# Layer 0's first MLP matmul by seven products of halves, sums in place of the raw weights, and one modulation vector handed to layer 1

## The chip, the cores and the metric

The kernel runs on one core of one Trainium2 chip. The metric is the device time of one execution in microseconds (us). The engines are TensorE (PE in the profile; PEld is its weight load), VectorE (DVE), ScalarE (ACT), GpSimd (POOL) and SyncE (SP), whose queue issues the weight transfers.

## The reference

Two layers act on 128 context tokens and 512 latent tokens, 640 in all, with a model width of 1024. Layer 0 mixes by attention, layer 1 by a gated delta rule; each then has a squared-ReLU MLP with 4096 hidden columns. Six modulation vectors a layer (shift, scale and gate, for the mixer and for the MLP) come from a conditioning vector, one set for context and one for latent tokens. Everything is float32.

```python
m = jax.nn.silu(cvec) @ w + b            # modulation: w is 1024 x 6144
def squared_relu_mlp(h, w1, w2):
    return jnp.square(jax.nn.relu(h @ w1)) @ w2
for layer in range(2):
    sh1, sc1, g1, sh2, sc2, g2 = modulation(c, mod_w, mod_b)
    x = x + g1 * mixer(rms_norm(x, norm1) * (1 + sc1) + sh1)
    x = x + g2 * squared_relu_mlp(rms_norm(x, norm2) * (1 + sc2) + sh2, mlp_w1, mlp_w2)
```

## The kernel before

Activations are stored transposed, features on partitions, the 640 tokens along the free axis in two halves of 320. A float32 product is three matmuls of parts rounded to fp32r: high by high, high by low and low by high (lines 245 to 247). The 16 activation tiles `act` hold the high and low parts of the normalised input.

`dense` multiplies by a weight matrix in groups of 512 output columns. A block of 128 columns and one half of the tokens takes 8 x 3 = 24 matmuls into a bank of PSUM (`dn` and `p1` by turns). Weights come in transfers of 1 MB for 256 columns, all 1024 rows (`fetch`, line 255), into two raw buffers by turns. `split_w` makes the high part by a ScalarE copy (line 228) and the low part by a VectorE subtraction (line 229) in four pairs of buffers, used in rotation: `hls`, named `t`, and the pair `wxh`, `wxl`.

Modulation is hidden under the matmuls. `mod_steps` is a generator: each step fetches 1 MB of `mod_w` and folds it on VectorE into two accumulators `ma` (line 190 for the first, line 192 for the others, four operations a step); after four steps eight matmuls (line 198, `pick`) sum over the partitions, and two transposes and two additions store the vector. `fill(n)` runs n such steps from the list `fillers`, and `dense` calls it at every weight fetch.

The program is issued from this code. In the part from layer 0's output projection on, the tile framework keeps the order by engine, except that it moves an instruction ahead where another has to wait by its own estimate; so what one loop yields is interleaved with what others yield.

The MLP goes through four quarters of 1024 hidden columns: `w1` for a quarter (hidden tiles `hh`, `hl` by `split_h`, lines 542 and 543), then `w2` for it, which adds into the residual (line 407). In layer 1 the second to fourth quarters of `w1` go through `seven`: per 256 columns the inputs and the weights are cut into 2 x 2 halves (features by tokens, columns by features), and Strassen's product in Winograd's form takes 7 products of 12 matmuls, 84, in place of 96. The input sums T1 to T4 are made once (`sums`). The weight sums S1 to S4 are made for each tile by `forms`, one step of it after every second product (`tile_of`); `kept` copies a partial product from PSUM (line 472), `put` adds the last one to it (line 482), and `ev7` applies the squared ReLU, on VectorE for one of four results (line 553) and on ScalarE otherwise (lines 555 and 556). Layer 0's MLP is plain `dense` in all quarters, with `fill=1` at each fetch: its seven pending vectors are layer 0's last, (0, 5), and layer 1's (1, 0) to (1, 5).

At the entry of each MLP the second half of the tokens is still being normalised: `sumsq` accumulates squares (line 299), a matmul by ones (line 306) sums them over partitions, and lines 383 to 395 scale and split.

Of the kernel before, what the change touches and what calls it, by code (L numbers as in the profile page):

```python
# [49 lines left out]
class Net:  # L50
# [211 lines left out]
    def dense_steps(self, w, row0, col0, ncol, xs, evac, tag=("dn", "dn"), fill=0, wide=(), size=4, between=None, early=None):  # L262


        for q in range(0, ncol, size * P):
# [4 lines left out]
            for i, (b, hf) in enumerate(steps):  # L270
                if b not in ws:
                    t = col0 + b * P
                    ws[b], ws[b + 1] = self.ahead.pop((w.tensor.name, row0, t), None) or self.fetch(w, row0, t)
                    self.fill(fill)
# [138 lines left out]
    def seven(self, pool):  # L413
# [10 lines left out]
        def sums():  # L424
            for k in range(4):
                b = []
                for z in (act(k, 0), act(k, 1), act(k + 4, 0), act(k + 4, 1)):
                    t = pool.tile([P, TH], F32, tag="c", name="b", bufs=4)
# [10 lines left out]
        def forms(w, col0):  # L439
# [5 lines left out]
            z = self.split_w(raw[:, :, 0:P], [P, NK, P])  # L445
            f["11"], f["12"] = ([y[:, 4 * i:4 * i + 4] for y in z] for i in range(2))
            yield f
            t = pool.tile([P, 2, 4, P], F32, tag="s0", name="s", bufs=1)
            nc.vector.tensor_tensor(out=t[:, 0], in0=a21, in1=a22, op=ALU.add)
            nc.vector.tensor_tensor(out=t[:, 1], in0=t[:, 0], in1=a11, op=ALU.subtract)  # L450
            z = self.split_w(t.rearrange("p a k c -> p (a k) c"), [P, NK, P])
            f["S1"], f["S2"] = ([y[:, 4 * i:4 * i + 4] for y in z] for i in range(2))
            yield f
            u = pool.tile([P, 2, 4, P], F32, tag="s1", name="s", bufs=1)
            nc.vector.tensor_tensor(out=u[:, 0], in0=a11, in1=a21, op=ALU.subtract)
            nc.vector.tensor_tensor(out=u[:, 1], in0=a12, in1=t[:, 1], op=ALU.subtract)
            z = self.split_w(u.rearrange("p a k c -> p (a k) c"), [P, NK, P])
            f["S3"], f["S4"] = ([y[:, 4 * i:4 * i + 4] for y in z] for i in range(2))
            yield f
            f["22"] = self.split_w(a22, [P, 4, P])  # L460
# [14 lines left out]
        def tile_of(f, nxt, out):  # L475
# [4 lines left out]
            def put(i, hf, ps, sb, op=ALU.add):  # L480
                c = pool.tile([P, TH], F32, tag="c", name="c", bufs=4)
# [15 lines left out]
            u3 = kept(a, "k4")  # L497
# [6 lines left out]
            put(1, 0, u3, c, ALU.subtract)  # L504
# [23 lines left out]
    def mlp(self, layer, xs, last, fill=0, between=None, early=None, fast=None):  # L528

        nc, tc = self.nc, self.tc  # L530
        with ExitStack() as c:
            hp = c.enter_context(tc.tile_pool(name="hp", bufs=16 if fast else 20))
            rp = c.enter_context(tc.tile_pool(name="rp", bufs=4))
            w1, w2 = self.i[f"mlp_w1_{layer}"], self.i[f"mlp_w2_{layer}"]
            for ch in range(4):
# [15 lines left out]
                def ev7(fb, hf, h):  # L551
                    if fb % 2 == 0 and hf == 0:
# [1174 lines left out]
```

## Time and profile before

| | us |
|---|---|
| median of three runs (lowest and highest) | 1848.47 (1845.96, 1849.6) |
| profiled execution | 1845.21 |
| span of its profile, first to last instruction | 1843.5 |
| mean granted TensorE clock of that span | 0.987 of full |
| TensorE, VectorE, ScalarE busy | 1754.1, 1208.7, 851.5 |
| first matmul of layer 1's second seven-product stage, and of the plain stage after it | 1521.33, 1570.61 |

All other numbers on the trace are from the profiled execution and count from the start of its span. Busy times are shares of the whole span, and the stages differ, so a stage has to be read by itself. In the timeline a matmul's length overlaps the next one's, since matmuls are pipelined; the distance of starts is the pace.

### The profile page before, as it was taken

The numbers are of one execution on the slowest core, as the hardware profiler recorded it, in microseconds if no ns is written. First come the engines' busy times: TensorE is split into PE (matmuls) and PEld (weight loads), VectorE is DVE, ScalarE is ACT, GpSimd is POOL, SyncE is SP. The second block draws the span as 40 slices with busy tenths as digits, with TensorE's granted clock in tenths as the row PEclk, the third lists the DMA queues.
The fourth block names the chain that finished last, engine by engine and source line by source line (L and its number), as shares of the span: only waits on it lengthen the run. The fifth ranks groups of instructions, "written<-read, shape, count | busy, mean of one in ns | idle before, by whom it ended". The sixth has DMA issues, their size and how long they took to land. (4 is left out here: it accounts for less than half of the span.)

```text
span 1843.5 us, 34925 instructions
## 1 busy us (share of the span) xinstructions
PE 1754.1 (95%) x14264; PEld 1648.8 (89%) x14264; DVE 1208.7 (66%) x2420; ACT 851.5 (46%) x1877; POOL 254.0 (14%) x252
## 2 busy tenths in 40 slices
PE   5899998899999999999989999999999999999999
PEld 4898876699999999999878888888899999999999
DVE  6766557478676667745687877776447757465562
ACT  4555576335223132233665666656645426254360
POOL 1233314111000000001331222222112000000000
PEclk8999998999999999999999999999999999999999
DMA  9201059324444344532223222222241212222131
GB/s 330 70 27 49 25 169 270 126 91 140 154 165 138 137 139 142 178 99 78 78 67 76 55 48 48 69 70 59 79 135 46 92 46 92 92 69 92 60 109 50
DMA packets 174992, 187.22 MB, mean 102 GB/s; under 512 B 48456, under 2 KB 152136, under 8 KB 174832
## 3 DMA queue, kind: packets, MB, share of 16 engines
q1 hardware_dynamic: 170272, 175.05, 30.2%
q0 software_dynamic: 1408, 5.41, 0.9%
q10 hardware_dynamic: 3152, 4.52, 0.7%
q8 instruction: 112, 1.84, 0.4%
q14 instruction: 48, 0.39, 0.1%
HBM read 170.97 MB, written 11.37 MB: 99 GB/s over the span
## 5 line engine op out<-in xcount | busy, mean ns | idle before, releaser
L228 ACT CAST t<-t 128x1024 fp32r<-128x1024 f32 (+1 forms) x151 | 152.7, 1013 | 250.3 <-PE p L246 152.5
L245 PE MATMUL dn<-t 128*128 128x320 f32 x792 | 252.6, 319 | 4.8 <-PEq L78 3.1
L246 PE MATMUL dn<-t 128*128 128x320 f32 x792 | 253.3, 320 | 1.3 <-DVE t L395 0.8
L247 PE MATMUL dn<-t 128*128 128x320 f32 x792 | 252.0, 318 | 0.0
L229 DVE TENSOR_TENSOR t<-t 128x1024 fp32r<-128x1024 f32 (+1 forms) x151 | 179.2, 1188 | 76.7 <-ACT t L228 76.5
L245 PEld LDWEIGHTS dn<-t 128*128 128x128 f32 x792 | 149.9, 189 | 9.1 <-issue 5.4
L246 PEld LDWEIGHTS dn<-t 128*128 128x128 f32 x792 | 149.9, 189 | 5.9 <-issue 2.5
L247 PEld LDWEIGHTS dn<-t 128*128 128x128 f32 x792 | 149.9, 189 | 3.3 <-issue 2.5
L246 PE MATMUL p<-hl,t 128*128 128x320 f32 x448 | 138.4, 309 | 0.0
L407 DVE SCALAR_TENSOR_TENSOR x<-p,t,x 128x192 f32<-128x192 f32 (+2 forms) x154 | 53.3, 386 | 128.5 <-PE p L247 128.5
L192 DVE SCALAR_TENSOR_TENSOR ma<-t,ma 128x1024 f32<-128x1024 f32 x98 | 123.3, 1279 | 13.7 <-DMA t<-in_mod_w_dram 13.7
L246 PE MATMUL dn<-hl,t 128*128 128x320 f32 x416 | 128.5, 309 | 0.0
L245 PE MATMUL p<-hh,t 128*128 128x320 f32 x392 | 121.1, 309 | 0.0
L247 PE MATMUL p<-hh,t 128*128 128x320 f32 x392 | 121.1, 309 | 0.0
L245 PE MATMUL dn<-hh,t 128*128 128x320 f32 x376 | 116.4, 310 | 0.0
L247 PE MATMUL dn<-hh,t 128*128 128x320 f32 x376 | 116.2, 309 | 0.0
L388 POOL TENSOR_TENSOR nt<-x,rs 128x320 f32<-128x320 f32 x30 | 31.0, 1048 | 567.7 <-ACT rs L308 538.0
L245 PE MATMUL p<-t 128*128 128x320 f32 x344 | 108.2, 314 | 0.0
L247 PE MATMUL p<-t 128*128 128x320 f32 x344 | 107.3, 312 | 0.0
L246 PE MATMUL p<-t 128*128 128x320 f32 x344 | 107.2, 312 | 0.0
L228 ACT CAST wxh<-t 128x1024 fp32r<-128x1024 f32 x43 | 45.1, 1048 | 103.0 <-PE p L246 60.0
L246 PEld LDWEIGHTS p<-hl,t 128*128 128x128 f32 x448 | 84.1, 188 | 0.0
(568 smaller groups left out, 5017.1 us busy)
## 6 DMA issues: line engine op xcount, KB each, us to landing
t<-in_mlp_w_dram SPq DMA_DIRECT2D x64, 1024.0 KB
t<-in_mod_w_dram SPq DMA_DIRECT2D x40, 1024.0 KB, 7.6
t<-in_w_qkv_dram SPq DMA_DIRECT2D x12, 1024.0 KB
t<-in_w_in_dram SPq DMA_DIRECT2D x9, 1024.0 KB, 5.4
w<-in_mod_w_dram SPq DMA_DIRECT2D x4, 2048.0 KB, 15.5
t<-in_w_out_dram SPq DMA_DIRECT2D x8, 1024.0 KB, 5.5
bias<-in_biasx_dram SPq DMA_DIRECT2D x8, 512.0 KB, 8.1
t<-in_w_z_dram SPq DMA_DIRECT2D x4, 1024.0 KB
```

Of the source, the lines that this page charges most:

```text
L192: nc.vector.scalar_tensor_tensor(out=acc[v], in0=wt[:, k], scalar=c, in1=acc[v], op0=ALU.mult, op1=ALU.add)
L228: nc.scalar.copy(hi, raw)
L229: nc.vector.tensor_tensor(out=lo, in0=raw, in1=hi.bitcast(F32), op=ALU.subtract)
L245: self.nc.tensor.matmul(ps, lhsT=hi[:, k, :], rhs=xh[:, ts_], start=(k == 0), stop=False)
L246: self.nc.tensor.matmul(ps, lhsT=hi[:, k, :], rhs=xl[:, ts_], start=False, stop=False)
L247: self.nc.tensor.matmul(ps, lhsT=lo[:, k, :], rhs=xh[:, ts_], start=False, stop=(k == NK - 1))
L388: nc.gpsimd.tensor_tensor(out=t, in0=xt[k][:, c], in1=rs[:, c], op=ALU.mult)
L407: nc.vector.scalar_tensor_tensor(out=xout[:, a:b], in0=ps[:, a - o:b - o], scalar=self.mod_vec(layer, idx, k, v), in1=xin[:, a:b], op0=ALU ...
```

## The change

Both layers now run the same MLP. Quarter 0 of `w1` is plain, with one modulation step at each fetch; in its `w2` stage the input sums are made, one k-pair at each fetch, and the other three quarters of `w1` go through `seven`. In layer 0 the modulation steps at `w2`'s fetches go by turns of 1, 1 and 2 and there are none in the seven-product stages; layer 0 makes the vectors (0, 5) and (1, 0) to (1, 4), and (1, 5) is made at the entry of layer 1's MLP, in quarter 0 of `w1`.

In `forms` the sums are written over the raw weights (only S1's operand has a buffer of its own, `s`), and the splits are grouped otherwise: a11 and a12 together, S1 alone, S2 and S4, then S3 and a22; before it was S1 with S2, S3 with S4, and a22 alone. In `tile_of` the last result now takes its partial product from PSUM and a kept copy of the other, so that three kept tags are used in place of four. `ev7` is always two ScalarE operations. Buffers move between pools: `c` has 3 in place of 4, `hp` of layer 0 has 16 in place of 20, and the pool of the normalisation is closed while `sv` is open and opened again for the last `w2`.

```diff
-                    self.fill(fill)
+                    fill() if callable(fill) else self.fill(fill)

...
-                    t = pool.tile([P, TH], F32, tag="c", name="b", bufs=4)
+                    t = pool.tile([P, TH], F32, tag=("c", "c", "c", "k1")[len(b)], name="b", bufs=(3, 3, 3, 1)[len(b)])

...
-            z = self.split_w(raw[:, :, 0:P], [P, NK, P])
-            f["11"], f["12"] = ([y[:, 4 * i:4 * i + 4] for y in z] for i in range(2))
+
+            def split(i, *names):
+                z = self.split_w(raw[:, :, i * P:(i + 1) * P], [P, NK, P])
+                for j, nm in enumerate(names):
+                    f[nm] = [y[:, 4 * j:4 * j + 4] for y in z]
+
+            split(0, "11", "12")
             yield f
-            t = pool.tile([P, 2, 4, P], F32, tag="s0", name="s", bufs=1)
-            nc.vector.tensor_tensor(out=t[:, 0], in0=a21, in1=a22, op=ALU.add)
-            nc.vector.tensor_tensor(out=t[:, 1], in0=t[:, 0], in1=a11, op=ALU.subtract)
-            z = self.split_w(t.rearrange("p a k c -> p (a k) c"), [P, NK, P])
-            f["S1"], f["S2"] = ([y[:, 4 * i:4 * i + 4] for y in z] for i in range(2))
+            t = pool.tile([P, 4, P], F32, tag="s", name="s", bufs=1)
+            for out, u, v, op in ((t, a21, a22, ALU.add), (a21, a11, a21, ALU.subtract), (a11, t, a11, ALU.subtract),
+                                  (a12, a12, a11, ALU.subtract)):
+                nc.vector.tensor_tensor(out=out, in0=u, in1=v, op=op)
+            f["S1"] = self.split_w(t, [P, 4, P])
             yield f
-            u = pool.tile([P, 2, 4, P], F32, tag="s1", name="s", bufs=1)
-            nc.vector.tensor_tensor(out=u[:, 0], in0=a11, in1=a21, op=ALU.subtract)
-            nc.vector.tensor_tensor(out=u[:, 1], in0=a12, in1=t[:, 1], op=ALU.subtract)
-            z = self.split_w(u.rearrange("p a k c -> p (a k) c"), [P, NK, P])
-            f["S3"], f["S4"] = ([y[:, 4 * i:4 * i + 4] for y in z] for i in range(2))
+            split(0, "S2", "S4")
             yield f
-            f["22"] = self.split_w(a22, [P, 4, P])
+            split(1, "S3", "22")
...
-                c = pool.tile([P, TH], F32, tag="c", name="c", bufs=4)
+                c = pool.tile([P, TH], F32, tag="c", name="c", bufs=3)

...
-            u3 = kept(a, "k4")
             put(1, 1, a, s5)
             product(d, f["S4"], x["22"], False, True)
             put(0, 1, d, u2)
             step()
             c = self.bank("p1")[:, 0:TH]
             product(c, f["22"], x["T4"], True, True)
-            put(1, 0, u3, c, ALU.subtract)
+            put(1, 0, a, kept(c, "k2"), ALU.subtract)
             step()
...
         return sums(), columns
-    def mlp(self, layer, xs, last, fill=0, between=None, early=None, fast=None):
+    def mlp(self, layer, xs, last, fill=0, between=None, early=None, room=None, back=None):
         nc, tc = self.nc, self.tc
         with ExitStack() as c:
-            hp = c.enter_context(tc.tile_pool(name="hp", bufs=16 if fast else 20))
+            hp = c.enter_context(tc.tile_pool(name="hp", bufs=16))
             rp = c.enter_context(tc.tile_pool(name="rp", bufs=4))
+            sv = c.enter_context(ExitStack())
             w1, w2 = self.i[f"mlp_w1_{layer}"], self.i[f"mlp_w2_{layer}"]
             for ch in range(4):
                 hs = {}
...
-                    if fb % 2 == 0 and hf == 0:
-                        nc.vector.scalar_tensor_tensor(out=h, in0=h, scalar=0.0, in1=h, op0=ALU.max, op1=ALU.mult)
-                    else:
-                        nc.scalar.activation(h, h, AF.Relu)
-                        nc.scalar.activation(h, h, AF.Square)
+                    nc.scalar.activation(h, h, AF.Relu)
+                    nc.scalar.activation(h, h, AF.Square)
                     split_h(fb, hf, h)
 
-                if ch and fast:
+                if ch:
                     columns(w1, ch * D, 4, ev7)
+                    fill2 = fill
                 else:
-                    self.dense(w1, 0, ch * D, D, xs, ev1, tag=("dn", "p1"), fill=fill, wide=(0,) if ch == 0 else (), early=early if ch == 0 else None)
-                    if fast:
-                        fast()
-                        sums, columns = self.seven(c.enter_context(tc.tile_pool(name="sv", bufs=1)))
-                        self.fillers.insert(0, sums)
-                self.dense(w2, ch * D, 0, D, hs, lambda k, hf, ts_, ps: last(k, hf, ps, ch), tag=("dn", "p1"), fill=1 if fast and not ch else fill,
+                    self.dense(w1, 0, 0, D, xs, ev1, tag=("dn", "p1"), fill=1, wide=(0,), early=early)
+                    room()
+                    sums, columns = self.seven(sv.enter_context(tc.tile_pool(name="sv", bufs=1)))
+
+                    def fill2():
+                        next(sums, None)
+                        fill()
+
+                if ch == 3:
+                    sv.close()
+                    if back:
+                        back()
+                self.dense(w2, ch * D, 0, D, hs, lambda k, hf, ts_, ps: last(k, hf, ps, ch), tag=("dn", "p1"), fill=fill2,
                            wide=(1,) if ch == 3 and between else (), between=between if ch == 3 else None)
-                if fast:
-                    self.fill(99)
 
 
 def attn_layer(n):
...
-            n.open_norm(cn)
-            n.modp = cn.enter_context(n.tc.tile_pool(name="mp", bufs=1))
+            n.modp = cn.enter_context(n.tc.tile_pool(name="mp", bufs=1, side="right"))
+            nn = ctx.enter_context(ExitStack())
+            n.open_norm(nn, side="right")
...
-            n.fillers += [n.mod_steps(l, j, "s1") for l, j in [(0, 5)] + [(1, j) for j in range(6)]]
+            n.fillers += [n.mod_steps(l, j, "s1") for l, j in [(0, 5)] + [(1, j) for j in range(5)]]
             def last0(k, hf, ps, ch):
...
-            n.mlp(0, xs, last0, fill=1, between=between0, early=(1, lambda: n.norm_half(x0, 0, 1, 1)))
+            turns = cycle((1, 1, 2))
+            n.mlp(0, xs, last0, fill=lambda: n.fill(next(turns)), between=between0, early=(1, lambda: n.norm_half(x0, 0, 1, 1)),
+                  room=nn.close, back=lambda: n.open_norm(nn, side="right"))
             def before():
+                nn.close()
+                cn.close()
-                cn.close()
...
+            n.modp = cn.enter_context(n.tc.tile_pool(name="mp", bufs=1, side="right"))
+            n.fillers.append(n.mod_steps(1, 5, "s1"))
             def last1(k, hf, ps, ch):
-            n.mlp(1, xs, last1, early=(1, lambda: n.norm_half(x2, 1, 1, 1)), fast=cn.close)
-            cn.close()
+            n.mlp(1, xs, last1, fill=lambda: n.fill(1), early=(1, lambda: n.norm_half(x2, 1, 1, 1)), room=cn.close)
```

Line numbers of the changed kernel are one or two higher around `seven` (`kept` is 473, `put` 483, relu and square 554 and 555, `hh` 544).

On ScalarE, one steady tile of a seven-product stage (the `w1` of layer 1), in the order before. `k` are the kept copies from the banks `dn` and `s`, `t<-s 128x1024` is the high part of two sums, `c` a result on its way to `hh`.

```order
L472 COPY k_18004<-dn 128x320
L542 CAST hh<-c 128x320
L228 CAST t<-s 128x1024
L472 COPY k_18019<-s_18006 128x320
L472 COPY k_18038<-dn 128x320
L555 ACTIVATE c<-c 128x320
L556 ACTIVATE c<-c 128x320
L228 CAST t<-s 128x1024
L542 CAST hh<-c 128x320
L555 ACTIVATE c<-c 128x320
L228 CAST t<-t 128x512
L556 ACTIVATE c<-c 128x320
```

The same engine and place in the changed kernel:

```order
L473 COPY k_19187<-dn 128x320
L555 ACTIVATE c<-c 128x320
L544 CAST hh<-c 128x320
L228 CAST wxh<-t 128x1024
L554 ACTIVATE c<-c 128x320
L555 ACTIVATE c<-c 128x320
L473 COPY k_19224<-dn 128x320
L544 CAST hh<-c 128x320
L228 CAST t<-s 128x512
L473 COPY k_19239<-s_19226 128x320
L554 ACTIVATE c<-c 128x320
L555 ACTIVATE c<-c 128x320
```

The copy of 512 elements now stands first among the sums (S1, from `s`) and the wide ones come from the raw buffer `t`; a relu and a square go with every result.

On VectorE at the entry of layer 1's MLP, before: L407 is the residual update of `w_out1`, L299 the sum of squares, L383 and L393 the normalisation.

```order
L407 SCALAR_TENSOR_TENSOR x_15998<-dn,t,x_15998 128x320
L299 TENSOR_TENSOR acc<-acc,sq 128x320
L407 SCALAR_TENSOR_TENSOR x_16000<-p_16342,t,x_16000 128x320
L299 TENSOR_TENSOR acc<-acc,sq 128x320
L383 SCALAR_TENSOR_TENSOR nt<-x_15986,t,rs 128x320
L393 TENSOR_SCALAR nt<-nt,t 128x320
```

And in the changed kernel:

```order
L299 TENSOR_TENSOR acc<-acc,sq 128x320
L190 TENSOR_SCALAR ma<-t 128x1024
L192 SCALAR_TENSOR_TENSOR ma<-t,ma 128x1024 x2
L407 SCALAR_TENSOR_TENSOR x_16180<-dn,t,x_16180 128x320
L299 TENSOR_TENSOR acc<-acc,sq 128x320
L407 SCALAR_TENSOR_TENSOR x_16182<-p_16524,t,x_16182 128x320
L299 TENSOR_TENSOR acc<-acc,sq 128x320
L192 SCALAR_TENSOR_TENSOR ma<-t,ma 128x1024
L383 SCALAR_TENSOR_TENSOR nt<-x_16168,t,rs 128x320
```

The first modulation step of (1, 5) now stands between the last residual updates, one operation of it directly ahead of the first normalisation (another L190 stands one row above this piece).

On TensorE, the picks of one of layer 0's vectors before, at the end of a half-block of `w1` (`p`), with the next block's matmuls (`dn`) behind them:

```order
L247 MATMUL p_6714<-t 128x320
L198 MATMUL s_6754<-ma,t 32x256 x8
L245 MATMUL dn<-t,wxh 128x320
L246 MATMUL dn<-t,wxh 128x320
L247 MATMUL dn<-t,wxl 128x320
```

And in the changed kernel the picks of a vector in the `w2` stage of quarter 2:

```order
L245 MATMUL dn<-hh,t 128x320
L198 MATMUL s_9384<-ma,t 32x256 x4
L246 MATMUL dn<-hl,t 128x320
L247 MATMUL dn<-hh,t 128x320
L245 MATMUL dn<-hh,t 128x320
L246 MATMUL dn<-hl,t 128x320
L247 MATMUL dn<-hh,t 128x320
L245 MATMUL dn<-hh,t 128x320
L246 MATMUL dn<-hl,t 128x320
L247 MATMUL dn<-hh,t 128x320
L198 MATMUL s_9384<-ma,t 32x256 x4
L245 MATMUL p_9429<-hh,t 128x320
```

The eight picks are now two groups of four inside and at the end of a half-block, eight matmuls apart. TensorE has 144 matmuls of 320 columns fewer in the whole program; the counts of SP and POOL are the same.

## Rows read from the trace of the kernel before

**Rows 1.** The page's first part: engine, busy us, share of the span, instructions.

```profile
PE 1754.1 (95%) x14264; PEld 1648.8 (89%) x14264; DVE 1208.7 (66%) x2420; ACT 851.5 (46%) x1877; POOL 254.0 (14%) x252
```

**Rows 2.** Windows: PE, PEld, DVE, ACT, POOL busy (count), granted clock, DMA share, GB/s.

```profile
460.00:860.00 400.00, 400.00 (x2780) 395.32 (x2779) 258.54 (x367) 107.13 (x177) 0.00 (x0) 1.00 0.43 141
1521.00:1571.00 50.00, 50.00 (x343) 50.00 (x342) 35.18 (x57) 34.13 (x67) 0.00 (x0) 1.00 0.31 98
```

**Rows 3.** TensorE's timeline at stage starts: start, length, instruction, idle before.

```profile
1521.33 0.46 PE L467 MATMUL dn<-t,wxh 128*128 128x320 f32 x2
...
1570.61 0.31 PE L245 MATMUL dn<-hh,wxh 128*128 128x320 f32 x1
...
1627.26 0.46 PE L467 MATMUL dn<-t,wxh 128*128 128x320 f32 x2
```

**Rows 4.** TensorE's timeline in layer 0's MLP: first picks of two successive vectors.

```profile
456.37 0.42 PE L198 MATMUL s<-ma,t 128*32 128x256 f32 x4
...
514.09 0.42 PE L198 MATMUL s<-ma,t 128*32 128x256 f32 x4
```

**Rows 5.** TensorE's timeline at both MLP entries: layer 0, then layer 1.

```profile
394.18 0.54 PE L306 MATMUL s<-acc,t 128*128 128x320 f32 x1
...
413.11 0.82 PE L306 MATMUL s<-acc,t 128*128 128x320 f32 x1 [2.29 <-DVE acc L299]
...
1390.39 0.51 PE L306 MATMUL s<-acc,t 128*128 128x320 f32 x1
...
1410.05 1.44 PE L306 MATMUL s<-acc,t 128*128 128x320 f32 x2 [3.04 <-DVE acc L299]
...
1450.93 0.31 PE L245 MATMUL dn<-t 128*128 128x320 f32 x1
```

**Rows 6.** VectorE by shape, 400 to 860 us: busy, mean ns, idle before.

```profile
L192 DVE SCALAR_TENSOR_TENSOR ma<-t,ma 128x1024 f32<-128x1024 f32 x95 | 119.5, 1279 | 12.2 <-DMA t<-in_mod_w_dram 12.2
...
L190 DVE TENSOR_SCALAR ma<-t 128x1024 f32<-128x1024 f32 x12 | 9.0, 750 | 3.9 <-PE s L198 3.9
```

**Rows 7.** Windows behind the two waits of rows 5.

```profile
413.00:423.00 10.00, 9.89 (x55) 9.50 (x56) 10.00 (x18) 7.50 (x16) 3.00 (x4) 0.83 0.53 179
1410.00:1420.00 10.00, 9.95 (x56) 9.55 (x57) 7.93 (x17) 6.14 (x16) 3.83 (x4) 0.83 0.34 107
```

**Rows 8.** ScalarE by shape, 1521 to 1571 us, a seven-product stage.

```profile
L542 ACT CAST hh<-c 128x320 fp32r<-128x320 f32 x14 | 6.4, 457 | 1.4 <-DVE c L553 1.3
...
L555 ACT ACTIVATE c<-c 128x320 f32<-128x320 f32 x11 | 5.1, 468 | 3.4 <-DVE c L482 3.4
L472 ACT COPY k<-dn 128x320 f32<-128x320 f32 x12 | 5.1, 422 | 7.2 <-PE dn L467 7.2
L556 ACT ACTIVATE c<-c 128x320 f32<-128x320 f32 x10 | 4.7, 470 | 0.1
L228 ACT CAST wxh<-t 128x1024 fp32r<-128x1024 f32 x4 | 4.2, 1051 | 1.5 <-PE p L467 1.4
...
L228 ACT CAST t<-t 128x512 fp32r<-128x512 f32 x3 | 1.8, 606 | 0.0
```

**Rows 9.** VectorE by shape, 1521 to 1571 us.

```profile
L543 DVE TENSOR_TENSOR hl<-c,hh 128x320 fp32r<-128x320 f32 x13 | 6.3, 486 | 1.8 <-ACT hh L542 1.8
L229 DVE TENSOR_TENSOR wxl<-t,wxh 128x1024 fp32r<-128x1024 f32 x4 | 4.9, 1218 | 0.0
...
L229 DVE TENSOR_TENSOR t<-t 128x512 fp32r<-128x512 f32 x3 | 2.1, 690 | 0.0
...
L482 DVE TENSOR_TENSOR c<-dn,k 128x320 f32<-128x320 f32 x4 | 1.9, 487 | 0.1
```

**Rows 10.** VectorE's timeline behind that stage's end.

```profile
1574.11 0.49 DVE L543 TENSOR_TENSOR hl<-c,hh 128x320 fp32r<-128x320 f32 x1 [0.34 <-ACT hh L542]
```

**Rows 11.** What line 192 waits for (us, times), and the modulation transfers (median us to landing).

```profile
  DMA t<-in_mod_w_dram: 13.7, 18
...
t<-in_mod_w_dram SPq DMA_DIRECT2D x40, 1024.0 KB, 7.6
```

More of the change, by code (lines that the diff above doesn't have):

```diff
@@ L1 @@
 import math
-from itertools import chain
+from itertools import chain, cycle
 from contextlib import ExitStack, contextmanager
```

## The prediction

> **What bounds the kernel now.** I read the page's first part, then busy time by windows, then single matmuls in TensorE's timeline, then VectorE and ScalarE by shape, and last the waits and transfers of the weights. The first part says that TensorE is busy for 95% of the span and VectorE for 66% [rows 1]. The windows say what that average hides: from 460 to 860 us, layer 0's MLP, TensorE is busy for 400.00 of 400 us, and from 1521 to 1571 us, a stage of layer 1 that already works with seven products, for 50.00 of 50, both at full clock [rows 2]. So inside both MLPs time is the number of matmuls, as long as VectorE, ScalarE and the weights keep up. The pace is read from two starts: the stage that begins at 1521.33 ends where a plain one begins, at 1570.61 [rows 3]. It holds 4 tiles of 7 products of 12 matmuls, 336, so one takes 49.28 / 336 = 0.1467 us. The plain stage after it (8 blocks, 2 halves, 24 matmuls: 384) and the next boundary end at 1627.26: 56.65 against 384 x 0.1467 = 56.32. The boundary loses 0.33 us; from the first number to the third one quarter is 105.93.
>
> **Matmuls removed.** Three quarters of layer 0's first matmul go from 384 matmuls to 336, 144 fewer in all: 144 x 0.1467 = -21.1 us. Nothing lies beside these, since TensorE has no idle time there; all of it is on the path, and this is also the floor.
>
> **New boundaries.** Layer 0 gets three transitions from seven products to plain, 0.33 us each by the quarter above: +1.0.
>
> **The vector that moves to layer 1.** Its TensorE part is the same in both places. Successive picks start at 456.37 and 514.09 [rows 4]: 57.72 for 384 matmuls, so 1.40 us a vector, subtracted in layer 0 and added in layer 1. Its VectorE part is new in layer 1's entry, where the normalisation of the other half is late already. The rows of the changed order there (two L190 and three L192 between L407, L299 and L383) are those that layer 0's entry has now, and the two entries can be compared in the trace of before. From the sums over partitions to the place of the first picks layer 0 takes 456.37 - 394.18 = 62.19 us and layer 1, without that work, 1450.93 - 1390.39 = 60.54 [rows 5]. I take the difference, +1.65 us; ends 0 (if the five operations fall into pauses) and 4.9 (2 x 0.75 + 3 x 1.28 - 0.4, all of them ahead of L383 [rows 6], the last term for one that lies behind).
>
> Part of the entry's cost is the clock. After TensorE's wait of 3.04 us at 1410.05 the next ten microseconds have a granted clock of 0.83, and after layer 0's wait of 2.29 us the same 0.83 [rows 5, 7]: what full clock (2.4 GHz) for two thirds of that window and half (1.2 GHz) for a third would make. The Trainium skill (TensorE: Matmul & The Clock Gate, What's actually happening) says that half clock is the resting state and that work releases it, which agrees with both rows. By its section Why this matters for your kernels a shorter pause can leave the clock whole; a window at 0.83 loses 0.17 x 10 = 1.7 us against full clock, and without that loss the sum would be about -18.1. The row with 2.29 us speaks against it, and I go by the row.
>
> **VectorE and ScalarE under seven products.** A tile is 84 matmuls, 12.32 us. By the changed order ScalarE has per tile 3 wide copies, 1 narrow, 4 kept, and 4 each of hh, relu and square: 3 x 1.05 + 0.61 + 4 x 0.42 + 4 x (0.457 + 0.468 + 0.470) = 11.0 us [rows 8]. VectorE has 3 wide splits, 1 narrow, 4 sums of weights (at the narrow split's 0.69), 4 additions and 4 hl: 3 x 1.22 + 0.69 + 4 x 0.69 + 4 x 0.487 + 4 x 0.486 = 11.0 [rows 9]. Both are under 12.32, with 1.3 us to spare, and the present tile has 10.1 and 11.5 by the same rows. The tightest chain is the pair with S2 and S4: its last reader, the sixth product, ends 6 x 1.76 = 10.56 us into a tile; the copy into the freed pair (1.05) and the subtraction (1.22) can be done about 13.0, and the third product of the next tile wants it at 12.32 + 3.52 = 15.84. 2.8 us are left. A kept k1 of the next tile has 0.8. I cost both at nothing; ends 0 and, if each tile of the 24 lost 1 us, +24.
>
> **The tail of each such stage.** The plain stage after it needs hl of the last block; in the present one it waits 0.34 us for hh at 1574.11 and TensorE runs on, since other blocks' matmuls stand ahead [rows 10]. The changed chain has one more copy (0.42), and a square on ScalarE in place of one operation on VectorE. With six tails, 0 to 0.6 each where that cover of ready matmuls ends, I take 0.1 each: +0.6.
>
> **Modulation under w2 alone.** Five of layer 0's six vectors now fall into the plain stages of w2: 20 steps at 16 weight fetches, by turns of 1, 1 and 2, where they had w1's stages too. A step is 4 operations of 1.28 us, 2 of a vector's 16 taking 0.75 [rows 6]. The changed order has, between the last hl ahead of each of the first three w2 stages and the first hl behind it, VectorE work of 52.7, 45.2 and 51.5 us by the durations of the rows (in the first of them, for example, 16.8 of modulation, 11.7 of the sums T1 to T4, 10.5 of low parts, 10.4 of residual updates), against about 56.3 + 3.5 of TensorE work in the same stretch. VectorE follows; it does not bound. But the picks now stand where the matmuls ahead of them may be done sooner than their data: the eight are broken into four and four between matmuls of a dn block. A mod transfer takes 7.6 us from issue to landing, and VectorE has waited 13.7 us in 18 places for the former [rows 11]. Five places are close by my count (the first pick in w2 of quarter 0, three picks later, the last weight tile of quarter 3). Each costs 0 to 1.5 us, the upper end being two waits of the present mean, 13.7 / 18 = 0.76; I take 0.3 each: +1.5.
>
> **Sum.** -21.1 + 1.0 + 1.65 + 0.6 + 1.5 = -16.4 us. The profiled execution took 1845.2 us (1843.5 of span and 1.7 around it); that makes 1828.8. It is 3.3 us below the median of the three runs, 1848.5, from which the sum gives 1832.1. I say 1831.
>
> **Rivals.** *No stalls at all*: the floor of -21.1 us with the boundaries inside it, 1824 to 1827. For it: TensorE's idle time in the windows is zero, with the modulation in them. Against: the entry of layer 1 has a row that says otherwise. *The squeeze*: VectorE, with five or six modulation steps in a w2 stage and the sums in the first, is late with the weights' low parts and with the picks; each of some 16 places loses 0.5 us on top, half of the gain: 1835 to 1843. For it: the 13.7 us of waits, each now under a stage with less room; against: VectorE's total is still below the stage's. *Nothing gained*: the same squeeze with 1 us in each of 16 places, 1845 to 1852. *The other side*: the chain of S2 and S4 (pair freed, copy, subtraction) ends later than the third product, in each of the 24 tiles of both layers. From 16.4 / 24 = 0.7 us a tile on nothing is left; at 1 us each the time is 1855, slower by 8. For it: both engines have 11.0 of 12.32 us, and this order has the pair rewritten in half of the time that the present one has; against: 2.8 us of room, and the stage now has ScalarE at 34.1 of 50 and VectorE at 35.2 by the window [rows 2]. *It does not do what it says*: 144 matmuls are gone from the order, so only a repeated stage could be behind that; next to nothing.
>
> **How the numbers follow.** Forecast (1827 to 1835) 0.68, no stalls 0.10, squeeze 0.14, nothing gained 0.04, other side 0.04. The range reaches from the floor, 1824, to the greater part of the squeeze, 1842. Below 0.2% (3.7 us) a measurement of this kernel cannot tell a change from none; the first three cases lie beyond it on the fast side: faster 0.92, same 0.04, slower 0.04.
>
> **What would show it.** Picks or not, TensorE without idle from layer 0's second quarter on; layer 0's second to fourth quarter at about 105.9 us plus 1.4 for each vector picked in it (one or two); the first waits of layer 1's entry near 2.3, 0.8 and 0.5 us in place of one of 3.04; product starts of 1.76 us apart in the tiles, with no gap in front of the third one. A gap there, of any size, in every tile makes the prediction wrong; so does one of layer 0's w2 stages of over 61 us (56.3, two vectors, 2 more), or waits for the low parts of weights (L229) on TensorE.

## The result, and the profile after

The changed kernel takes 1826.74 us (median of four runs, 1824.25 to 1828.45), the kernel before 1849.03 beside it: a ratio of 0.9879, with a 95% interval of 0.9858 to 0.9900, some 22 us. Timed a second time (label `again`, below) the ratio is 0.9900 (0.9884 to 0.9915), some 18.5 us; the two intervals overlap. Much of the scatter goes with TensorE's granted clock (the share of its full speed), which differs from execution to execution: a straight line of time against granted clock, through 60 executions of before and 8 of the changed kernel (the 8 timed here and in `again`), puts the two 18.6 us apart at equal clock (an estimate from these runs). The profiled executions differ by 17.0 us of span, 1843.5 and 1826.5. The forecast was 1831, from a sum of -16.4 us.

The page's first part after; columns as in [rows 1]:

```profile
PE 1737.9 (95%) x14120; PEld 1629.0 (89%) x14120; DVE 1275.3 (70%) x2528; ACT 923.5 (51%) x2037; POOL 254.3 (14%) x252
```

144 TensorE instructions are gone, as forecast; VectorE and ScalarE have 67 and 72 us more to do. Windows after, with the columns of [rows 2]: layer 0's MLP as there, its first `w2` stage (the one with the sums T1 to T4), and its first seven-product stage.

```profile
460.00:860.00 400.00, 398.21 (x2749) 390.87 (x2738) 320.18 (x491) 177.32 (x329) 5.71 (x7) 1.00 0.40 131
474.90:532.50 57.60, 57.60 (x403) 56.82 (x402) 49.42 (x80) 12.47 (x19) 0.00 (x0) 1.00 0.39 128
532.60:581.80 49.20, 49.20 (x337) 49.20 (x336) 38.23 (x58) 37.44 (x74) 0.00 (x0) 1.00 0.30 97
```

VectorE went from 258.54 to 320.18 us of 400, and TensorE stays full but for 1.8 us. The stage starts of layer 0 in TensorE's timeline (seven products, then `w2`, and so on):

```profile
474.80 0.31 PE L245 MATMUL dn<-hh,t 128*128 128x320 f32 x1
...
532.53 0.46 PE L468 MATMUL dn<-t 128*128 128x320 f32 x2
...
581.81 0.31 PE L245 MATMUL dn<-hh,t 128*128 128x320 f32 x1
...
640.32 0.46 PE L468 MATMUL dn<-t 128*128 128x320 f32 x2
...
689.63 0.31 PE L245 MATMUL dn<-hh,t 128*128 128x320 f32 x1
...
749.53 0.46 PE L468 MATMUL dn<-t 128*128 128x320 f32 x2
...
798.82 0.31 PE L245 MATMUL dn<-hh,t 128*128 128x320 f32 x1
```

The three seven-product stages take 49.28, 49.31 and 49.29 us, the pace of [rows 3] without a gap. The `w2` stages between them take 57.73, 58.51 and 59.90: 56.32, a vector's 1.40 for one, one and two picks, 0.33 for the boundary in the later two, and 0.46 and 0.45 more, in which the picks are split into two groups. In the last `w2` stage is the one wait inside this MLP (in `again` there is a second one, of 0.47 us):

```profile
600.94 0.42 PE L198 MATMUL s<-ma,t 128*32 128x256 f32 x4
...
602.29 0.42 PE L198 MATMUL s<-ma,t 128*32 128x256 f32 x4
...
831.34 0.42 PE L198 MATMUL s<-ma,t 128*32 128x256 f32 x4 [1.72 <-DVE ma L192]
```

Cut at the same instructions, the differences of the two profiled executions are these. Attention ends at the entry's wait (413.11 in [rows 5], 416.14 after); layer 0's MLP runs from there to the wait of the delta layer's entry (881.75, 866.37), the delta layer to the first sum over partitions of layer 1's MLP (1390.39, 1370.87), and the rest to the end of the span.

| us | before | after | difference | forecast |
|---|---|---|---|---|
| attention, layer 0 | 413.11 | 416.14 | +3.03 | 0 |
| MLP of layer 0 | 468.64 | 450.23 | -18.41 | -19.7 |
| delta layer and `w_out1` | 508.64 | 504.50 | -4.14 | 0 |
| from layer 1's MLP entry | 453.11 | 455.63 | +2.52 | +3.35 |

The forecast column is its own terms put in their places: -21.1 + 1.0 - 1.40 + 0.3 + 1.5 for layer 0, 1.40 + 1.65 + 0.3 for layer 1. The two MLPs together are -15.9 against -16.4. What was not forecast is the delta layer. TensorE's waits in that stretch, of before and then of the changed kernel (total us, times, longest; only the rows whose releaser is "issue", time in which the engine waited for nothing that the profile shows):

```profile
PE L L1351 <- issue: 3.3, 3, 2.1
...
PE L L1382 <- issue: 1.5, 1, 1.5
```

```profile
PE s L1228 <- issue: 0.2, 1, 0.2
```

4.9 us before, 0.2 after. Where they lie, in TensorE's timeline of before:

```profile
984.39 0.55 PE L1351 MATMUL L<-rp,y 32*32 32x32 f32 x41
985.63 0.54 PE L1351 MATMUL L<-rp,y 32*32 32x32 f32 x39 [0.69 <-issue]
```

A burst of 80 matmuls of 32 x 32, 41 of them in 0.55 us, stops in the middle though the profile shows nothing that it waits for.

### The profile page after: what moved, and what is told of

It is laid out like the page before. It is cut to its first block, busy times and chain, and to the rows that moved or that the text cites. A ratio compares the mean times of both kernels' runs of the same rounds, so it can differ in the third digit from the quotient of the medians.

```text
span 1826.5 us, 34931 instructions
## 1 busy us (share of the span) xinstructions
PE 1737.9 (95%) x14120; PEld 1629.0 (89%) x14120; DVE 1275.3 (70%) x2528; ACT 923.5 (51%) x2037; POOL 254.3 (14%) x252
## 4 chain that ended last, share of the span: by engine, by line
PE 56%; DVE 13%; issue 6%; ACT 3%; DMA 2%; POOL 1%; SPq 0%; DVEq 0%; ACTq 0%; POOLq 0%
PE dn L468 7%; PE dn L245 6%; PE dn L246 6%; PE dn L247 6%; PE p L247 5%; PE p L245 5%; PE p L246 5%; PE p L468 5%; PE s L468 5%; DVE t L229 1%; DVE ma L192 1%; PE p L1432 1%; DMA t<-in_w_out_dram 1%; PE p L1441 1%; DVE at L1292 1%
## 5 line engine op out<-in xcount | busy, mean ns | idle before, releaser
L228 ACT CAST t<-t 128x1024 fp32r<-128x1024 f32 x169 | 176.6, 1048 | 248.2 <-PE p L246 137.7
L229 DVE TENSOR_TENSOR t<-t 128x1024 fp32r<-128x1024 f32 x169 | 207.6, 1230 | 55.9 <-ACT t L228 54.8
L245 PE MATMUL dn<-t 128*128 128x320 f32 x648 | 209.1, 323 | 4.7 <-PEq L78 3.1
L246 PE MATMUL dn<-t 128*128 128x320 f32 x648 | 209.6, 324 | 1.3 <-DVE t L395 0.8
L247 PE MATMUL dn<-t 128*128 128x320 f32 x648 | 208.4, 322 | 0.0
L245 PEld LDWEIGHTS dn<-t 128*128 128x128 f32 x648 | 123.5, 191 | 9.4 <-issue 5.4
L246 PEld LDWEIGHTS dn<-t 128*128 128x128 f32 x648 | 123.6, 191 | 5.9 <-issue 2.5
L407 DVE SCALAR_TENSOR_TENSOR x<-p,t,x 128x192 f32<-128x192 f32 (+2 forms) x154 | 53.2, 384 | 106.6 <-PE p L247 106.6
L247 PEld LDWEIGHTS dn<-t 128*128 128x128 f32 x648 | 123.6, 191 | 3.4 <-issue 2.5
L228 ACT CAST wxh<-t 128x1024 fp32r<-128x1024 f32 x49 | 51.3, 1048 | 92.1 <-PE p L246 47.7
L407 DVE SCALAR_TENSOR_TENSOR x<-dn,t,x 128x320 f32<-128x320 f32 (+1 forms) x86 | 44.8, 524 | 59.9 <-PE dn L247 49.8
L775 POOL TENSOR_TENSOR p<-p,smx 128x640 f32<-128x640 f32 (+1 forms) x48 | 63.8, 1338 | 114.1 <-DVE smx L774 98.7
L246 PEld LDWEIGHTS dn<-hl,t 128*128 128x128 f32 x416 | 78.1, 188 | 1.0 <-issue 0.8
L245 PEld LDWEIGHTS p<-hh,t 128*128 128x128 f32 x392 | 73.6, 188 | 0.4 <-ACT t L228 0.4
```

Of the source, the lines that this page charges most:

```text
L228: nc.scalar.copy(hi, raw)
L229: nc.vector.tensor_tensor(out=lo, in0=raw, in1=hi.bitcast(F32), op=ALU.subtract)
L245: self.nc.tensor.matmul(ps, lhsT=hi[:, k, :], rhs=xh[:, ts_], start=(k == 0), stop=False)
L246: self.nc.tensor.matmul(ps, lhsT=hi[:, k, :], rhs=xl[:, ts_], start=False, stop=False)
L247: self.nc.tensor.matmul(ps, lhsT=lo[:, k, :], rhs=xh[:, ts_], start=False, stop=(k == NK - 1))
L407: nc.vector.scalar_tensor_tensor(out=xout[:, a:b], in0=ps[:, a - o:b - o], scalar=self.mod_vec(layer, idx, k, v), in1=xin[:, a:b], op0=ALU ...
```

## The experiments

**The two kernels again.** Nothing is edited in `again` (the changed kernel) and `before2`.

> The changed kernel once more, unaltered. Its first profile differs from that of before by -17.0 us: +3.0 in the attention stage, -18.4 in layer 0's MLP, -5.1 in the delta layer (4.65 of it are waits that the trace puts down to 'issue'), +3.5 in layer 1's MLP; the medians differ by -22.3. Theory COUNT: the two MLPs make the whole difference; attention and the delta layer come out as it happens in each execution, so this profile has the MLPs at -18.4 and +3.5 against before within 0.3 us, and any values between 0 and 5 us of 'issue' waits; timed difference -15 +- 3. Theory LAYOUT: the changed program has lost the 'issue' waits for good; under 0.5 us of them in this profile, and a timed difference of -20 +- 2.

> The kernel before once more, unaltered. Both theories: a ratio of 1.000 within 0.002. COUNT: 'issue' waits on TensorE in the delta layer anywhere from 0 to 5 us. LAYOUT: they are there again with 4 to 6 us (0.7, 1.6, 0.5 and 2.1 us at lines 1351 and 1382 in the first profile).

`before2`: ratio 0.9998 (0.9986 to 1.0009). The "issue" waits come back in it at the same four matmuls, with lengths within 0.4 us of the first, 4.84 us in all, and `again` has 0.18:

```profile
PE L L1351 <- issue: 3.0, 3, 1.7
...
PE L L1382 <- issue: 1.8, 1, 1.8
```

So they belong to the program, not to the execution; COUNT, which let them fall anywhere, is wrong on that, and LAYOUT right. The timed -18.5 lies in LAYOUT's range and half a microsecond outside COUNT's, so the times alone would not decide between them. Layer 0's MLP is 468.63 and 450.93, the rest from layer 1's MLP on 453.04 and 455.81: -14.9 for the two MLPs. Attention ends at 412.43 and 410.77: its +3.03 was the execution's own.

**Layer 0 plain again** (`l0_plain`).

```diff
-                if ch:
+                if ch and layer == 0:
+                    self.dense(w1, 0, ch * D, D, xs, ev1, tag=("dn", "p1"))
+                    fill2 = fill
+                elif ch:
...
```

The part left out keeps layer 0 from making the input sums T1 to T4.

> The changed kernel with layer 0's second to fourth quarter of w1 plain again; all else as changed (layer 1 with sums in place, modulation under w2 alone, vector (1, 5) in layer 1). COUNT: 144 matmuls come back, 21.1 us, less three boundaries of 0.3: layer 0's MLP 20 us longer than the changed one's, the whole 20 us above the changed kernel, 1 to 3 us above before in the sum of the MLPs. Rival MODULATION: what layer 0 pays for its squeezed modulation goes with the seven products, and the plain stages give ScalarE and VectorE room again; the wait of 1.72 us ahead of the last picks is gone and the whole is only 18 above the changed one.

Ratio 1.0000 (0.9990 to 1.0011): with the 144 matmuls back the whole gain is gone. Layer 0's MLP takes 468.76 us, 18.5 and 17.8 more than in the two profiles of the changed kernel. That is less than 20, as rival MODULATION has it: there is no wait ahead of the last picks, one of 0.80 us ahead of an earlier vector's, and four of the five vectors are picked in one piece (eight picks together, not four and four). With plain stages, and without the input sums, the picks have more room; which of the two gives it was not told apart. "Issue" waits: 2.63 us.

**Layer 0 alone** (`l0_alone`): layer 1's `forms`, `kept` and `ev7` as before, and

```diff
-            n.fillers += [n.mod_steps(l, j, "s1") for l, j in [(0, 5)] + [(1, j) for j in range(5)]]
+            n.fillers += [n.mod_steps(l, j, "s1") for l, j in [(0, 5)] + [(1, j) for j in range(6)]]
-            turns = cycle((1, 1, 2))
+            turns = cycle((1, 2))
```

> Layer 0 as changed, but layer 1's MLP as before (grouping of the sums, four kept copies, VectorE for one square of four) and vector (1, 5) made in layer 0 as before, its steps at w2's fetches by turns of 1 and 2. COUNT: layer 0's MLP -18.4 + 1.4 = -17 us against before, or up to 2 less gain if 24 steps press VectorE more than 20; layer 1's MLP as before within 0.3 us. Rival: the grouping of the sums in layer 1 is worth something by itself; then the seven-product stages of layer 1 are longer here than the changed ones' 49.28 us.

Ratio 0.9893 (0.9879 to 0.9907), layer 0's MLP 452.52 us, -16.1, a little under the expected -17. Layer 1's first seven-product stage, here with the old grouping:

```profile
1500.95 0.46 PE L495 MATMUL dn<-t,wxh 128*128 128x320 f32 x2
...
1550.23 0.31 PE L245 MATMUL dn<-hh,wxh 128*128 128x320 f32 x1
```

49.28 us, as in the changed kernel (1504.51 to 1553.79). The sums in place, three kept copies and the squares on ScalarE neither cost nor gain anything there; whether layer 0's buffers would fit without them was not tried. One expectation failed: from the first sum over partitions of layer 1's MLP to the end it is 454.4 us, 1.3 more than before, where at most 0.3 was expected. All of it is in the entry, 75.90 us against 74.6 though no vector is picked there, and the clock behind its wait of 3.04 us is lower than the 0.83 of [rows 7] (columns of [rows 2]):

```profile
1388.40:1398.40 10.00, 10.00 (x47) 9.61 (x48) 7.94 (x17) 6.34 (x16) 3.83 (x4) 0.69 0.35 107
```

**How near ScalarE is** (`act1` and `act2`, one execution each): the copy of S2 and S4 made again. The argument named `again` is 1 in `act1` and 2 in `act2` for this copy, and 0 for all others; the lines that pass it on are left out.

```diff
-        nc.scalar.copy(hi, raw)
+        for _ in range(1 + again):
+            nc.scalar.copy(hi, raw)
...
```

> The changed kernel with the copy of S2 and S4 made twice in every tile: 1.05 us more of ScalarE per tile, 11.0 + 1.05 = 12.05 of 12.32 us, in the chain of the pair that the forecast found the tightest (2.8 us of room). Theory ROOM: the seven-product stages stay at 49.3 us (up to 49.6). Rival NO ROOM: the chain ends later than it was worked out, and each stage is 4 x 1 = 4 us longer.

> The same copy made three times: 13.1 us of ScalarE per tile of 12.32. Theory ROOM: now ScalarE bounds the stage and a tile takes what ScalarE needs, 13.1 us; a stage 52.4 us, 3.1 more, six stages 19 us more, and the whole is at before's time. Rival: the durations overlap (a start follows the last end sooner than the sum says), ScalarE needs only 12.5, and the stages stay under 50.5.

The first is as ROOM has it: stages of 49.28 us but for one in layer 0 with 49.89, and the wait that shows first is on a kept copy, where the forecast counted 0.8 us of room, not on the pair of S2 and S4:

```profile
667.75 0.41 PE L470 MATMUL dn<-t20h,wxh 128*128 128x320 f32 x1 [0.34 <-ACT k L475]
```

The second refutes the 19 us. Layer 1's last three quarters grew by 2.4, 0.7 and 0.6 us, layer 0's MLP in total not at all (450.89). ScalarE's load per tile is not the bound. By the code only three tiles of a stage make sums for a next one, so an excess of 0.8 us a tile would add up to 2.4 a stage; that most of this fits the room of the chains is argued, not shown. In this program the framework also put `w2`'s first matmul of each stage ahead of the last products, so the stage's end is not the changed kernel's. What remains shows there, where the second of `w2`'s matmuls waits for the last `hh`:

```profile
1556.46 0.41 PE L246 MATMUL dn<-hh,wxh 128*128 128x320 f32 x1 [1.64 <-ACT hh L546]
```

**Moving the delta layer in the instruction stream** (`pad40`, `pad96`, one execution each): in layer 0's MLP the first matmul of a half-block is issued four times more, in its first 10 half-blocks (`pad` 40) or 24 (`pad` 96).

```diff
...
+            for _ in range(4 if k == 0 and self.pad > 0 else 0):
+                self.pad -= 1
+                self.nc.tensor.matmul(ps, lhsT=hi[:, k, :], rhs=xh[:, ts_], start=True, stop=True)
```

> The changed kernel with 40 matmuls of layer 0's first w1 group made twice (4 for each of ten half-blocks): 40 x 0.147 = 5.9 us more there, and every TensorE instruction behind them 80 instructions further on. Theory LAYOUT: TensorE's 'issue' waits in the delta layer's bursts of small matmuls depend on where the burst stands in the instruction stream; they come back with 1 to 5 us, at other lines than before. Rival: they went for another reason (the order of the transfers around them), and stay under 0.5 us.

> 96 matmuls made twice in place of 40 (4 for each of 24 half-blocks of layer 0): 14.1 us more in layer 0, and 192 instructions' shift for the delta layer. LAYOUT: 'issue' waits of another sum and at other places than with 40 (2.4 us) and with none (0.2 us), between 0 and 5 us. Rival: the sum stays at 2.4 us, at the same lines.

With 40 the "issue" waits are back, 2.43 us; with 96 there are none.

```profile
PE L L1360 <- issue: 2.4, 2, 2.0
```

Against the expectation they are not at another line: line 1360 of `pad40` is line 1351 of before, and both waits stand one matmul earlier in the delta layer than two of before's. What is fixed is the place in the program. By the matmul records of the traces, counted from the program's start, the waits of the changed kernel, `l0_alone`, `pad40`, `turns211`, `e0022`, `e0211` and `v15_l0` stand behind 6557 to 6559 matmuls or behind 10376 and 10377, whatever work has come to lie there; in before and `l0_plain` it is 6681 and 6685, 10499 and 10503, and before has two more, one of them 127 matmuls behind its first. Between transpositions such a place costs 0.2 us, inside a burst 0.2 to 2.1. Where the bursts stand in the instruction stream therefore decides the waits, as LAYOUT has it.

The traces also hint at the cause. All 20 "issue" waits of the delta layer, in eleven profiles, end 2.2 to 2.8 us after the start of a 16 KB packet of DMA queue 8, whose kind is "instruction". This is the one ahead of before's wait at 985.63 (982 to 984 us: packets, MB, share of 16 engines):

```profile
q8 instruction: 1, 0.02, 3.5%
```

That reads as TensorE waiting for its next instructions; no run changed how they are fetched, so it is not shown.

Seven programs with 0.2 us or less of these waits have 503.8 to 508.0 us in the delta layer. The rest goes with the clock: 503.8 to 504.5 us at a mean granted clock of 0.997 in that stretch, 505.4 to 505.6 at 0.993 and 508.0 at 0.990. The clock is the execution's own, 0.997 in the first profile of before and 0.983 in the second.

**Modulation one fetch earlier** (`turns211`).

```diff
-            turns = cycle((1, 1, 2))
+            turns = cycle((2, 1, 1))
```

> The changed kernel with layer 0's modulation steps at w2's fetches by turns of 2, 1, 1 in place of 1, 1, 2: the same 20 steps, the later ones of each vector one fetch earlier. The changed kernel's profile has one wait of 1.65 to 1.72 us ahead of the last vector's picks, and the picks that are split into four and four cost 0.46 us more than the whole ones. Theory LATE DATA: the wait comes from the two steps at the last but one fetch; it falls under 0.5 us, two vectors' picks are whole again, and layer 0's MLP (between the second halves' sums over partitions of its entry and of the next) is 450.2 - 1.7 - 2 x 0.46 = 447.6 us, 448 to 449 with losses. Rival FULL VECTORE: the first w2 stage gets six steps beside the sums, 52.7 + 5.1 us against 59.8, and the wait appears there in its place; the MLP stays at 450.

Ratio 0.9858 (0.9838 to 0.9879), median 1821.73; layer 0's MLP 448.64 us, 1.6 and 2.3 less than in the two profiles of the changed kernel. LATE DATA holds in the main. Three of the five vectors' picks in `w2` are whole; the wait is smaller, not gone:

```profile
824.34 0.42 PE L198 MATMUL s<-ma,t 128*32 128x256 f32 x4 [1.05 <-DVE ma L192]
```

This is the fastest version of the study; its interval overlaps the changed kernel's first one (0.9858 to 0.9900), and ends just below the second (0.9884 to 0.9915).

**Modulation out of the entry** (`e0022`, and `e0211` with `(0, 2, 1, 1)`), on top of turns 2, 1, 1.

```diff
+            entry = iter((0, 0, 2, 2))
...
-                    self.dense(w1, 0, 0, D, xs, ev1, tag=("dn", "p1"), fill=1, wide=(0,), early=early)
+                    self.dense(w1, 0, 0, D, xs, ev1, tag=("dn", "p1"), fill=lambda: self.fill(next(entry)), wide=(0,), early=early)
```

> The kernel with turns 2, 1, 1 in layer 0's w2 stages (448.6 us of layer 0's MLP), and with the modulation steps of quarter 0 of w1, in both layers, not one at each of its four fetches but none at the first two and two at each of the others: none stands beside the normalisation at the entry. Layer 1's entry (from the first sum over partitions to the first w2 matmul, less 1.40 for the picks) takes 75.9 to 76.2 us in four profiles with the vector there, whatever the clock did (0.83 or 1.00 in the ten us behind the wait), 74.5 and 74.6 in two of before. Theory VECTORE: the five operations of the first step make it longer; without them the entry is 74.6, layer 0's as well about 1.5 less, the waits on lines 395 and 385 are gone, and the whole is 3 us below the kernel with turns 2, 1, 1, about 0.9845 of before. Rival CLOCK: the difference is the half clock behind the first wait, which is drawn anew in each execution; the entry stays at 75 to 76.5. Risk named ahead: four steps in the second half of the stage bring the picks late, 1 to 4 us in front of w2 in each layer.

> The same with turns of 0, 2, 1, 1 in quarter 0 of w1: two steps at the second fetch, whose VectorE operations the order puts behind the first half's normalisation and between the second half's. VECTORE: the waits ahead of the first blocks go, some come back behind them; the entry is 74.6 to 75.5, the whole 1 to 3 us below the kernel with turns 2, 1, 1. CLOCK: no change.

Ratios 0.9881 (0.9864 to 0.9897) and 0.9884 (0.9867 to 0.9901): no gain over turns 2, 1, 1 alone. The times look slower, but the intervals overlap; in the profiles layer 0's MLP is 1.8 and 4.7 us longer and the part from layer 1's MLP on the same within 0.2. At layer 1's entry `e0022` has lost the waits for lines 395 and 385, and has late picks in their place:

```profile
1389.65 0.54 PE L306 MATMUL s<-acc,t 128*128 128x320 f32 x1 [2.91 <-DVE acc L299]
...
1438.49 0.42 PE L198 MATMUL s<-ma,t 128*32 128x256 f32 x4 [0.89 <-DVE ma L192]
```

The entry takes 77.21 us; less 1.40 for the picks, 0.89 of wait and some 0.4 for the split it is 74.5, before's 74.5 to 74.6. VECTORE is right about the cause, and the named risk took the gain: in layer 0 the wait is 2.09 us and the entry 2.8 us longer (5.6 in `e0211`, 4.2 of them in two waits).

**All vectors in layer 0** (`v15_l0`).

```diff
-            turns = cycle((1, 1, 2))
+            turns = cycle((2, 1))
-            n.modp = cn.enter_context(n.tc.tile_pool(name="mp", bufs=1, side="right"))
-            n.fillers.append(n.mod_steps(1, 5, "s1"))
```

(and `range(6)` for layer 1's vectors, as in `l0_alone`).

> The changed kernel, but vector (1, 5) made in layer 0 with the others, 24 steps at w2's 16 fetches by turns of 2 and 1; nothing of modulation in layer 1. Theory VECTORE: layer 1's entry is rid of the five operations and of the late picks, 74.5 to 74.6 us from the first sum over partitions to the first w2 matmul (77.3 with the vector, 1.40 of them its picks); layer 0's MLP takes 448.6 + 1.4 = 450 to 451; the whole is 1 to 2 us below the kernel with turns 2, 1, 1 (0.9858). Rival SQUEEZE: 24 steps leave VectorE no room in layer 0's w2 stages; layer 0's MLP takes 452 to 454 by waits ahead of picks and at the delta layer's entry, and the whole is no better than the changed kernel, 0.988 to 0.990.

Ratio 0.9888 (0.9867 to 0.9908). The entry is 74.64 us, as forecast:

```profile
1372.80 0.51 PE L306 MATMUL s<-acc,t 128*128 128x320 f32 x1
...
1447.44 0.31 PE L245 MATMUL dn<-hh,wxh 128*128 128x320 f32 x1
```

But layer 0's MLP is 452.27 us, as SQUEEZE has it, by a wait for the last weight tile of `w2`:

```profile
835.60 0.42 PE L245 MATMUL dn<-hh,wxh 128*128 128x320 f32 x1 [2.48 <-ACT wxh L228]
```

## Why the prediction was right, step by step

**The time by itself** says little. 1826.74 lies just below the main case (1827 to 1835) and in the range of the rival *no stalls at all* (1824 to 1827), but that rival's mechanism did not happen: layer 1's entry and the late picks cost what is listed below. The time came out lower because the delta layer lost waits of 4.65 us that the sum did not have. That part was luck; the main term and its path were right.

**Matmuls and boundaries**: right. The stages are 49.28 to 49.31 us, and `l0_plain` gives all of it back. The boundaries cost 0.33 each.

**The vector in layer 1**: right in cause and nearly in size. From the first sum over partitions to the first `w2` matmul the changed kernel takes, less 1.40 for the picks, 75.9 and 76.1 us, and before 74.6 and 74.5: +1.3 to 1.6, forecast +1.65. The first wait is near layer 0's of 2.29 [rows 5], and two behind it are of 0.83 and 0.47, as the forecast said:

```profile
1389.54 0.54 PE L306 MATMUL s<-acc,t 128*128 128x320 f32 x1 [2.05 <-DVE acc L299]
...
1402.02 0.41 PE L246 MATMUL dn<-t,wxh 128*128 128x320 f32 x1 [0.83 <-DVE t L395]
...
1403.64 0.42 PE L246 MATMUL dn<-t,wxh 128*128 128x320 f32 x1 [0.47 <-DVE t L385]
```

`e0022` takes the vector's steps away from the normalisation and `v15_l0` takes the vector out of the entry; they get 74.5 and 74.6. `l0_alone` has no vector there either and gets 75.90, with a lower clock. So entries have to be compared at the same clock: at 0.83 behind the first wait it is 75.9 with the vector, and 74.6 without in before and in `v15_l0`.

**The clock**: the windows behind this wait, in the changed kernel and in `again`, with the columns of [rows 7]:

```profile
1389.50:1399.50 10.00, 9.96 (x56) 9.80 (x57) 10.00 (x18) 7.61 (x16) 3.60 (x4) 0.83 0.54 179
```

```profile
1386.00:1396.00 10.00, 8.80 (x56) 8.38 (x57) 10.00 (x18) 7.46 (x16) 3.59 (x4) 1.00 0.53 182
```

At almost the same wait (2.05 and 2.24 us) one execution fell to half clock for a part of the window (0.83) and the other did not (1.00). The section of the Trainium skill by which a shorter pause can leave the clock whole (TensorE: Matmul & The Clock Gate, Why this matters for your kernels) agrees with the second and not with the first. The sum by it, -18.1, was wrong for both: the entry is 77.32 us with the half clock and 77.53 without. VectorE is busy for 10.00 of 10 us in both, and at full clock TensorE waits 1.15 us more for it, at 1391.82. That the half clock costs nothing holds only where VectorE sets the pace: in `l0_alone`, with VectorE at 7.94 of 10 us and TensorE at 10.00, a clock of 0.69 in place of 0.83 goes with 1.3 us more.

**VectorE and ScalarE under seven products**: right to cost them at nothing in the changed kernel, whose two profiles lose 0.1 us at most in any stage. The rival on the other side was much further off than its 24 tiles x 1 us made it: `act2` puts 2.1 us a tile into that very chain, and the 24 tiles lose 3.7 us by it. The kept copy, not the pair, is the first to wait, and its small room is real: in `pad96`, whose edit lies outside these stages, two of them take 50.53 and 50.63 us.

```profile
1650.38 0.42 PE L472 MATMUL dn<-t20h,t 128*128 128x320 f32 x1 [1.08 <-ACT k L477]
```

**The tails**: mis-sized at +0.6, they cost nothing. A quarter of layer 1 is 105.88 us now, 105.93 before.

**Picks and weight tiles**: forecast +1.5 for five places. The three later `w2` stages take 0.46, 0.45 and 2.20 us more than matmuls, picks and boundaries explain (the last one, 67.55 us up to the wait of the delta layer's entry, against before's 63.62, a vector's 1.40 and a boundary's 0.33), 3.1 in all, 1.72 of it the one wait. Counted so, the last stage is 60.3 us, just under the 61 that the prediction named as a sign of being wrong. With 3.1 in place of 1.5 and no tails, layer 0's terms add up to the measured -18.4. The direction was right and its cause, as `turns211` shows; the term was half its size, since the split itself had been given no price. The last weight tile of quarter 3, named as close, waited in `v15_l0` with four steps more (2.48 us), and not here.

**What the sum did not have**: the delta layer, costed at 0 since its order is the same, gained 4.1 us in the profiles, and 7.2 in the second pair. 4.65 of that are "issue" waits, by where the code lies. With them the sum would be -21; the two timed differences are -22 and -18.5, and 18.6 us is the estimate at equal clock. In the first pair the clock of this stretch is 0.997 in both profiles, and the waits account for the 4.1 us within 0.5; in the second pair it is 0.983 before and 0.993 after, and the difference is 2.5 us more than the waits. Why TensorE stops at such a place of the program stays open.

## What to carry to other kernels

Where a stage's windows show TensorE full, take its pace from two starts and count matmuls; that gave the two MLPs here within 1.5 us, with errors of either sign among the small terms. Then ask of background work not whether its engine has room in total but where its result is consumed: 5 us of VectorE moved by one fetch were worth 2 us, and work taken out of a crowded entry came back as late picks. A difference of a few microseconds in a stage that the change does not touch can still come from the change, by the place of bursts of tiny instructions in the program; a second profile of each kernel tells that from chance. Compare code lines by their text, not their number, when two kernels differ, and two stretches only with the granted clock of each beside them.

## What the runs showed that was not expected

The pauses in bursts of 32 x 32 matmuls come again within 0.4 us each in a second execution of the same program, and go from 4.9 to 0.2, 2.6, 2.4 and 0 us when the program in front of them changes. Half clock behind a wait of about 2 us is drawn anew by each execution: at layer 1's entry the window was at 0.83 in one profile of the changed kernel and at 1.00 in the other.
